# A seven-product MLP with more groups: partial sums seeded into PSUM, kept in DRAM between pieces, and more low parts made by adding transfers

## The chip, the cores and the metric

The kernel runs on one core of one Trainium2 chip. A core has a matrix engine (TensorE, in profiles PE, with PEld for its weight loads), a vector engine (VectorE, DVE), an activation engine (ScalarE, ACT), a general engine (GpSimd, POOL) and a queue engine (SyncE, SP) that here issues most transfers. TensorE adds its products into PSUM, eight banks of 128 x 512 float32 words; everything else lives in SBUF or in DRAM. The metric is the device time of one execution in microseconds; smaller is better.

## The reference

The program is one inference step of a transformer layer for two groups of 128 tokens each, prompt (s = 0) and sample (s = 1), with a model width of 2048:

```
h = RMSNorm(x) * (1 + scale1) + shift1
q_A|k_A|v_A|q_B|k_B|v_B|gate_A|gate_B = split(h @ w_in)
x = x + gate1 * ((sigmoid(gate_A) * (o_A @ w_br_a) + sigmoid(gate_B) * (o_B @ w_br_b)) @ w_out)
h2 = RMSNorm(x) * (1 + scale2) + shift2
x = x + gate2 * (square(relu(h2 @ w_up)) @ w_down)
```

The six shift, scale and gate vectors are `silu(cond) @ w_ada + b_ada`, with one condition vector for each token group. `o_A` and `o_B` are two attentions with 128 cached keys each. `w_up` is 2048 x 8192 and `w_down` 8192 x 2048: the MLP is over half of the work. All inputs and outputs are float32.

## The kernel before

Each weight tile is 128 x 1024 float32 words, 512 KB, and is loaded once. To keep float32 accuracy, every operand is split into a high part (what TensorE's fp32r format holds) and a low part (the rest), and a product is three matmuls: high x high, high x low, low x high. The high part of a weight tile is a copy by ScalarE (`prep_hi`, through `copy`, line 93), the low part a subtraction by VectorE (`prep`, line 241). A few tiles, listed in `LO_DMA`, get their low part otherwise: ScalarE writes the negated high part and a transfer from POOL's queue adds the weight to it in SBUF (`minus_plus`, lines 247 and 248).

The work is a list of 456 steps, `wsteps`, in the order in which TensorE runs them. Steps 0 to 71 are the first columns of `w_in` (nine units of 512 columns, cut along the contraction into the CHUNKS 2, 2, 2, 4, 6 of its 16 tiles, so a unit comes back in each chunk); 72 to 135 the gates; 136 to 167 the branches; 168 to 199 `w_out`; 200 to 215 the first two column tiles of `w_up`. Then come eight pieces. A piece is a *pair*, two column tiles of `w_up` (16 steps; pair p from step 184 + 32p), and a *down* stage, four units of 512 output columns over the two column tiles of the piece (16 steps; down p from 232 + 32p, and down 7 from 440). The pair of the next piece stands ahead of a piece's down stage. A plain step is twelve 128x512 matmuls. Down stage 6 is steps 424 to 439, down stage 7 is 440 to 455.

Within a pair, the eight positions are contraction blocks of 256 rows. A block can be done plainly, in two steps of twelve matmuls, or as a *group of seven products* (a Strassen scheme over 2 x 2 blocks; the two token groups are its rows): an x step and a y step with 21 matmuls in all. `FAST` lists which positions do the latter. A group needs sums of weight tiles (t, u and YB) and their splits, made by `prep_x` and `prep_y` on VectorE and ScalarE. The seven accumulators take all eight banks together with Z, and at the pair's end VectorE adds them up (line 1229).

The down sums of a unit n over the eight pieces are held in SBUF (`dsum[n]`). After each piece the accumulated part is added by VectorE (line 1269), or, where `SUM_DMA` says so, copied by ScalarE and added by a transfer (line 1273). Before the last piece, `gate_sum` multiplies the sum by the gate g2 and adds it to the residual x1 (lines 1250 and 1251); the last piece's part is added by `resid` (lines 916 and 917) and written out.

A *dot* (line 1339) is a column of `silu(cond) @ w_ada` computed on VectorE: a 128 x 1024 tile of the transposed weights times a broadcast condition (`cB`), summed along the row, one operation for each token group. `DOTS2` are the steps after which the 32 tiles of gate g2 are worked on. `gate_rows` transposes the column of dots on TensorE (line 1352), writes it to DRAM, and `gate_bc` reads it back as a broadcast.

The order of every engine's work is what the program text emits step by step, in `run`: first the loads that are due (up to `RUN` steps past the step, each weight `LOAD` = 4 steps earlier still), then the preparation of weights up to `LOOK` steps ahead, then the step's matmuls, then what is listed after that step in `cal`. Each engine works through its own queue in order. Tiles come from one pool of `GEN` buffers of 128 x 1024 words, and a new tile waits for the last reader of the old one.

Of the kernel before, what the change touches and what calls it, by code (L numbers as in the profile page):

```python
# [18 lines left out]
P = 128  # L19
# [11 lines left out]
GEN = 48  # L31
# [15 lines left out]
LOOK = "652422234122454433223333332123333453344534333554455544344534333543324554444555556665556644444333333333332222122312344544555434333333342344333334333323445566643344456656433344434444445455564546555553444554322466554554433333333434334533333333333654544332334455643444555653315536554523333334543233333332223323365455455443222212233432443334434642333334444544534434333333333325434222223333434444444434555642255242433444442233554442233242223342112224442233345544"  # L47
RUN = "300000000000010212223333322222222221111122244455544355434445554334554445555775654544345434444445665543321222222212444444444444442222222232223344444455544544444444555454454466677755566555554543365434343355445756644443566664333312222234552332223333334545332333333333322211133333332233311101234434433332332112444444442454322211333343334323233334544422742222212223445554422333233322222211222333333435767445344121210002232000233455555566567556433435335553333334"
CONST_AT = [67, 70]
XL_DMA = []  # L50
ADA_AT = [None, 4, 13, 16, 21, 36, 32]
XS_AT = {1: 13, 2: 18, 3: 29}
POST = {('kvA', 0): [67, 70, 75], ('qA', 0): [70, 73, 78], ('qA', 1): [72, 74, 80], ('kB', 0): [77, 86, 90], ('qB', 0): [82, 84, 93], ('kB', 1): [87, 92, 95], ('qB', 1): [90, 93, 96]}
JOBS = [[79, 80, 80, 87, 93], [81, 83, 88, 90, 93], [87, 87, 89, 90, 96], [93, 93, 96, 102, 105], [96, 97, 100, 105, 112], [102, 103, 107, 112, 123], [105, 107, 111, 118, 123], [112, 115, 118, 121, 123]]
SS_AT = [41, 57, 73, 75, 135, 139]
T_AT = [4, 4]
PREP_IN = [6, 4]
DOTS = [33, 39, 42, 45, 47, 48, 49, 50, 53, 55, 55, 55, 60, 65, 69, 70, 73, 75, 80, 84, 90, 91, 92, 93, 95, 100, 101, 103, 103, 104, 108, 110, 111, 112, 115, 118, 120, 122, 123, 124, 126, 127, 128, 129, 130, 132, 133, 134, 137, 138, 138, 143, 144, 145, 147, 150, 153, 157, 159, 160, 166, 167, 170, 172, 173, 174, 175, 176, 178, 178, 179, 183]
DOTS2 = [230, 232, 234, 235, 236, 237, 240, 243, 255, 263, 265, 269, 270, 288, 300, 300, 306, 328, 328, 331, 333, 334, 358, 360, 362, 364, 368, 368, 391, 391, 395, 399]
STAT_AT = [-1, 0, 10, 11]  # L60
T_PAIR = [[10, 8], [6, 8], [8, 10], [5, 7], [10, 13], [8, 9], [12, 11]]
P_PAIR = [[5, 2], [2, 4], [3, 5], [-1, 3], [5, 8], [3, 3], [7, 4]]
M_TE = (3,)
M_AT = [1, 3, 8]
FLIP = 1
P_UP = [2, 2]
T_UP = [7, 5]
# [4 lines left out]
def tile_hybrid_step(ctx: ExitStack, tc: tile.TileContext, a):  # L72
# [25 lines left out]


    cols = cp.tile([P, 164], F32, name="cols")  # L100
    act.dma_start(cols, a["cols"])
    xnT = [G(f"xnT{g}").rearrange("p (k s t) -> p k s t", k=4, s=2) for g in range(4)]
    for g in range(4):
        sync.dma_start(xnT[g].rearrange("p k s t -> p (k s t)"), a["xT"][g])
# [1405 lines left out]
```

## Time and profile before

| | |
|---|---|
| median of 3 runs | 1329.3 us (1329.23 to 1330.28) |
| profiled execution: span from its first to its last instruction | 1327.5 us |
| TensorE matmuls busy | 1314.7 us, 6414 instructions |
| VectorE busy | 1179.5 us |
| ScalarE busy | 796.3 us |
| HBM read, written | 365.58 MB, 8.16 MB |

The profiled execution has no time of its own beside its span; the median of the runs is 1.8 us longer, which is what lies around the span. In the page's first part each engine has its busy time, share and count of instructions. In the second the span is cut into 40 slices and each digit is a share in tenths. A row of a group reads: line, engine, operation, output <- inputs, shape, count | busy time in us, mean ns of one | idle time of the engine before it and what ended that. A row of a timeline begins with the start in us and the duration. A row of waits reads: who <- for whom: us in total, times, longest. A row of windows has the stretch, its length, then busy time and instruction count of PE, PEld, DVE, ACT and POOL, the granted clock, the share of the transfer engines and GB/s. A matmul's duration is longer than the distance between two of them, since they are pipelined.

### The profile page before, as it was taken

How to read it: one execution, taken by the hardware profiler on the slowest of the kernel's cores; microseconds unless marked ns; L12 is line 12 of the kernel's file. 1: busy time of each engine (PE TensorE's matmuls, PEld its weight loads, DVE VectorE, ACT ScalarE, POOL GpSimd, SP SyncE). 2: the span in 40 equal slices, each digit the busy share in tenths (PEclk: the TensorE clock that was granted, in tenths of full speed). 3: DMA queues.
4: the chain of work that ended last, by engine and by line, in shares of the span. 5: the costliest groups of instructions: out<-in, count | busy, mean ns of one | idle time of the engine just before them, and what ended most of it. 6: DMA issues, size and time to landing. Idle time of an engine off the chain costs nothing.

```text
span 1327.5 us, 18042 instructions
## 1 busy us (share of the span) xinstructions
PE 1314.7 (99%) x6414; PEld 1066.7 (80%) x6415; DVE 1179.5 (89%) x1529; ACT 796.3 (60%) x973; POOL 49.9 (4%) x61
## 2 busy tenths in 40 slices
PE   8999999999999999999999999999999999999998
PEld 4777788788888878888888888888888888878886
DVE  4588999988898999999779998998999999989595
ACT  5634443467655546645677766767767567676560
POOL 0000000511000000000000000000000000000000
PEclk9999999999999999999999999999999999999999
DMA  9999997978589999996568956988969597788962
GB/s 372 408 409 409 409 387 278 389 263 272 188 310 351 359 390 331 375 370 239 191 229 262 302 222 229 276 290 276 278 223 298 203 305 248 273 224 283 312 208 100
DMA packets 147546, 389.62 MB, mean 294 GB/s; under 512 B 51712, under 2 KB 52928, under 8 KB 147456
## 3 DMA queue, kind: packets, MB, share of 16 engines
q1 hardware_dynamic: 144160, 377.11, 79.0%
q0 software_dynamic: 3152, 11.27, 4.3%
q8 instruction: 50, 0.82, 0.2%
q14 instruction: 40, 0.33, 0.1%
q10 hardware_dynamic: 144, 0.08, 0.0%
HBM read 365.58 MB, written 8.16 MB: 282 GB/s over the span
## 4 chain that ended last, share of the span: by engine, by line
PE 94%; DMA 4%; DVE 1%; ACT 0%; POOL 0%; issue 0%; SPq 0%; ACTq 0%
PE acc L291 17%; PE acc L293 17%; PE acc L292 17%; PE Q L1129 6%; PE Q L1131 6%; PE Q L1130 6%; PE acc L394 4%; PE acc L395 4%; PE acc L396 4%; DMA araw<-in_w_pair 3%; PE ps_ada L308 2%; DMA raw<-in_w_in 1%; PE Z L1129 1%; PE Z L1131 1%; PE Z L1130 1%; PE ps_S L719 1%
## 5 line engine op out<-in xcount | busy, mean ns | idle before, releaser
L241 DVE TENSOR_TENSOR wL<-raw,wH 128x1024 fp32r<-128x1024 f32 x379 | 449.9, 1224 | 62.4 <-ACT wH L93 58.0
L93 ACT ACTIVATE wH<-raw 128x1024 fp32r<-128x1024 f32 (+1 forms) x395 | 394.5, 1044 | 129.5 <-PE acc L396 21.5
L394 PE MATMUL acc<-wH,hH 128*128 128x512 f32 x276 | 109.1, 395 | 0.0
L396 PE MATMUL acc<-wH,hL 128*128 128x512 f32 x276 | 107.5, 390 | 0.0
L395 PE MATMUL acc<-wL,hH 128*128 128x512 f32 x276 | 107.5, 390 | 0.0
L291 PE MATMUL acc<-wH,hH 128*128 128x512 f32 x256 | 101.3, 396 | 0.0
L293 PE MATMUL acc<-wH,hL 128*128 128x512 f32 x256 | 99.7, 390 | 0.0
L292 PE MATMUL acc<-wL,hH 128*128 128x512 f32 x256 | 99.7, 389 | 0.0
L1339 DVE CUSTOM_DVE_ANT_0 junk<-aT,cB,cols 128x1024 bf16<-128x1024 f32 x56 | 71.7, 1286 | 0.0
L1339 DVE CUSTOM_DVE_ANT_0 aT<-aT,cB,cols 128x1024 f32<-128x1024 f32 x56 | 71.4, 1281 | 0.2
L93 ACT ACTIVATE tH<-t 128x1024 fp32r<-128x1024 f32 x32 | 33.9, 1060 | 51.9 <-DVE t L1184 44.5
L394 PEld LDWEIGHTS acc<-wH,hH 128*128 128x128 f32 x276 | 51.8, 188 | 13.6 <-issue 2.9
L396 PEld LDWEIGHTS acc<-wH,hL 128*128 128x128 f32 x276 | 51.8, 188 | 11.0
L395 PEld LDWEIGHTS acc<-wL,hH 128*128 128x128 f32 x276 | 51.9, 188 | 10.3
L293 PEld LDWEIGHTS acc<-wH,hL 128*128 128x128 f32 x256 | 48.1, 188 | 10.1
L291 PEld LDWEIGHTS acc<-wH,hH 128*128 128x128 f32 x256 | 48.1, 188 | 9.8 <-ACT wH L93 0.4
L292 PEld LDWEIGHTS acc<-wL,hH 128*128 128x128 f32 x256 | 48.1, 188 | 9.4
L93 ACT ACTIVATE uH<-raw 128x1024 fp32r<-128x1024 f32 x32 | 34.0, 1063 | 30.0 <-DVE raw L1189 29.0
L1235 ACT ACTIVATE up<-up 128x1024 f32<-128x1024 f32 x28 | 29.7, 1062 | 28.3 <-DVE up L1229 27.9
L308 PE MATMUL ps_ada<-araw,cpad 128*32 128x256 f32 x640 | 39.3, 382 | 2.6 <-DMA araw<-in_w_pair 2.5
L93 ACT ACTIVATE fTa<-pTa 128x2048 uint16<-128x2048 uint16 x16 | 40.5, 2534 | 2.1 <-PE acc L293 1.5
L1184 DVE TENSOR_TENSOR t<-raw 128x1024 f32<-128x1024 f32 x32 | 39.1, 1221 | 2.9 <-PE Q L1131 1.7
(641 smaller groups left out, 3291.7 us busy)
## 6 DMA issues: line engine op xcount, KB each, us to landing
raw<-in_w_in SPq DMA_DIRECT2D x133, 512.0 KB, 9.5
raw<-in_w_down SPq DMA_DIRECT2D x128, 512.0 KB, 5.7
araw<-in_w_pair SPq DMA_DIRECT2D x80, 512.0 KB, 10.0
aT<-in_w_gT SPq DMA_DIRECT2D x64, 512.0 KB, 6.8
raw<-in_w_up SPq DMA_DIRECT2D x64, 512.0 KB, 5.1
raw<-in_w_upF SPq DMA_DIRECT2D x64, 512.0 KB, 5.3
aT<-in_w_adaT SPq DMA_DIRECT2D x48, 512.0 KB, 9.9
raw<-in_w_out SPq DMA_DIRECT2D x32, 512.0 KB, 10.3
```

The source lines that it names most:

```text
L93: act.activation(out, in_, AF.Copy)
L241: dve.tensor_tensor(st["lo"], st["raw"], st["hi"].bitcast(F32), op=OP.subtract)
L291: pe.matmul(acc[tb], sh, wh[:, k, :], start=f, stop=False)
L292: pe.matmul(acc[tb], sh, wl[:, k, :], start=False, stop=False)
L293: pe.matmul(acc[tb], sl, wh[:, k, :], start=False, stop=l)
L394: pe.matmul(acc[tb], sh, wh[:, k, :], start=kt == 0 and k == 0 and not held, stop=False)
L395: pe.matmul(acc[tb], sh, wl[:, k, :], start=False, stop=False)
L396: pe.matmul(acc[tb], sl, wh[:, k, :], start=False, stop=last and k == 1 and not hold)
L1129: pe.matmul(acc, stat[0], hi, start=f, stop=False)
L1130: pe.matmul(acc, stat[0], lo, start=False, stop=False)
L1131: pe.matmul(acc, stat[1], hi, start=False, stop=l)
L1339: dve.tensor_tensor_reduce(out, box["raw"], cB[s, tag], 1.0, dst if second else baT[:, part, fb:fb + 1], OP.mult, OP.add, dst)
```

## The change

- Each of the seven pairs gets six groups of seven products (positions 0, 2, 3, 5, 6, 7): 42 groups in place of 32.
- The down units 1, 2 and 3 no longer add to a sum in SBUF. Between pieces their sums are written to DRAM by POOL's queue (up to piece 5), read back by SP's queue, and copied by ScalarE into the two PSUM banks of the unit (`seed`) before its matmuls, which then add to them. The last two pieces hand the sum over in SBUF. Unit 0 is added by VectorE as before, and only it goes through `gate_sum`.
- In the input projection, the units of chunks 3 and 4 (but the two that stay open) are seeded likewise from their partial sums.
- The high part of a weight is made one step ahead of its low part (`prep_a`, `prep_b`, HI_AHEAD), also in the groups; high and low parts of transposed tiles are made a step apart (JOIN_LO).
- `LO_DMA` has 35 entries in place of 10. One, 230, is the x step of a group, which makes its own parts in `x_hi` and `x_lo`; 34 are plain steps.
- The silu of the condition is computed once, at the start, and kept in DRAM; `cB` is read from there.
- The g2 dots are ordered by down unit, and each unit's gate is transposed and broadcast by itself (`gate_row2`, `gate_bc2`, through POOL's queue). Sixteen of the 32 dots now stand at steps 424 to 444.
- Some small constants move into two general buffers (`early`), and `GEN` grows from 48 to 50. The step lists (LOOK, RUN, DOTS, POST, JOBS and others) are new.

```diff
-GEN = 48
+GEN = 50
-DOTS1 = [11, 15, 27, 29, 29, 30, 32, 35]
+DOTS1 = [26, 26, 29, 36, 39, 40, 41, 42]
-FAST = {1: (0, 3, 7), 2: (0, 4, 5, 7), 3: (0, 2, 4, 5, 7), 4: (0, 2, 4, 5, 7), 5: (0, 3, 4, 5, 7), 6: (0, 2, 5, 6, 7), 7: (0, 1, 3, 5, 7)}
-SUM_DMA = [5, 6, 11, 13, 16, 19, 21, 23, 25]
+FAST = {1: (0, 2, 3, 5, 6, 7), 2: (0, 2, 3, 5, 6, 7), 3: (0, 2, 3, 5, 6, 7), 4: (0, 2, 3, 5, 6, 7), 5: (0, 2, 3, 5, 6, 7), 6: (0, 2, 3, 5, 6, 7), 7: (0, 2, 3, 5, 6, 7)}
+SUM_BACK = 8
+SEED_IN = {3: -1, 4: 0}
+SEED_N = (1, 2, 3)
+HI_AHEAD = 1
+JOIN_LO = 1
+SEED_AT = 3
+GATE2_USE = 3
+ROW_AT = [5, 5, 9, 5]
-LO_DMA = [89, 107, 131, 176, 184, 233, 292, 314, 319, 404]
+LO_DMA = [88, 106, 116, 131, 165, 180, 184, 196, 218, 224, 230, 232, 250, 251, 256, 282, 283, 288, 314, 315, 320, 329, 346, 347, 352, 378, 379, 384, 392, 410, 416, 442, 443, 449, 450]
...
-ADA_AT = [None, 4, 13, 16, 21, 36, 32]
+ADA_AT = [None, 5, 13, 16, 21, 37, 32]
-DOTS2 = [230, 232, 234, 235, 236, 237, 240, 243, 255, 263, 265, 269, 270, 288, 300, 300, 306, 328, 328, 331, 333, 334, 358, 360, 362, 364, 368, 368, 391, 391, 395, 399]
+DOTS2 = [234, 237, 240, 266, 269, 272, 298, 301, 329, 330, 332, 363, 364, 367, 397, 398, 424, 426, 426, 428, 429, 431, 431, 432, 432, 436, 439, 439, 440, 441, 444, 444]
...
+    act.activation(crow[:, 1, :], crow[:, 0, :], AF.Sigmoid)
+    pool.tensor_tensor(crow[:, 1, :], crow[:, 0, :], crow[:, 1, :], op=OP.mult)
+    pool.dma_start(silu, crow[:, 1, :])
...
-    prep_next = [0]
+    prep_next = [0, 0]
     def prep_to(end):
-        while prep_next[0] < min(len(wsteps), end):
-            prep(wsteps[prep_next[0]])
-            prep_next[0] += 1
+        for q, (ahead, fn) in enumerate(((HI_AHEAD, prep_a), (0, prep_b))):
+            while prep_next[q] < min(len(wsteps), end + ahead):
+                fn(wsteps[prep_next[q]])
+                prep_next[q] += 1
...
+    def seed(box, src):
+
+        box["acc"] = [bank("acc", pacc) for _ in range(2)]
+        for tb in range(2):
+            copy(box["acc"][tb], src[:, tb, :])
...
+            seed_step = len(wsteps) - nk // 2 + SEED_IN[c] if c in SEED_IN and j >= 2 else None
+            start_steps(u, k0, nk, c > 0 and j < 2, c < ends and j >= nf - 2, seed_step)
...
-    def unit(w, c0, ktiles, stat, evac, key, order="both"):
+    def unit(w, c0, ktiles, stat, evac, key, seed_from=None):
...
+        if seed_from:
+            at(len(wsteps) - SEED_AT, lambda: seed(box, seed_from()))
...
+            def x_hi(b=b):
+                b["X"] = b["x"].pop("raw")
                 b["XH"] = G("XH", F32R)
-                copy(b["XH"], b["x"]["raw"])
+                copy(b["XH"], b["X"])
+
+            def x_lo(b=b):
+                b["XL"] = G("XL", F32R)
+                dve.tensor_tensor(b["XL"], b["X"], b["XH"].bitcast(F32), op=OP.subtract)
...
+            def y_split(b=b):
+                for n, v in (("t", b["t"]), ("u", b["Y"])):
+                    b[n + "H"], b[n + "L"] = G(n + "H", F32R), G(n + "L", F32R)
+                    copy(b[n + "H"], v)
+                    dve.tensor_tensor(b[n + "L"], v, b[n + "H"].bitcast(F32), op=OP.subtract)
...
+    def sum_back(p, n):
+        dsum[n] = G(f"dsum{n}").rearrange("p (s n) -> p s n", s=2)
+        sync.dma_start(dsum[n].rearrange("p s n -> p (s n)"), sum_mem[p - 1, n])
+
     def down_unit(p, n):
+        seeded = p > 0 and n in SEED_N
+        if seeded and p < last:
+            load_at(len(wsteps) - SUM_BACK, lambda: sum_back(p, n))
+
         def evac(acc):
-            by_pool = 4 * p + n in SUM_DMA
-            if p == 0 or by_pool:
+            whole = p == 0 or seeded
+            if whole and p != last:
                 part = G(f"dsum{n}").rearrange("p (s n) -> p s n", s=2)
             for s in range(2):
                 if p == last:
                     out_s(acc, n, s)
-                elif p == 0 or by_pool:
+                elif whole:
                     copy(part[:, s, :], acc[s])
                 else:
                     dve.tensor_tensor(dsum[n][:, s, :], dsum[n][:, s, :], acc[s], op=OP.add)
-            if p == 0:
+            if n in SEED_N and p < last - 1:
+                sum_mem[p, n] = dp.tile([P, 1024], F32, name=f"sm{p}{n}")
+                pool.dma_start(sum_mem[p, n], part.rearrange("p s n -> p (s n)"))
+            elif whole and p != last:
                 dsum[n] = part
-            elif by_pool:
-                pool.dma_start(dsum[n], part, accum_op=OP.add)
...
+    def gate_row2(n):
+
+        ps = bank("ps_gr")
+        pe.transpose(ps[0:8, 0:P], g2col[n].rearrange("p s k -> p (s k)"), ident)
+        row = sp.tile([P, 512], F32, name="grow", tag="S", bufs=2)[0:8, 0:P]
+        copy(row, ps[0:8, 0:P])
+        grow["g2", n] = dp.tile([8, P], F32, name=f"gr_g2{n}")
+        pool.dma_start(grow["g2", n], row)
+
+    def gate_bc2(n):
+
+        gbc["g2", n] = G(f"g2_{n}").rearrange("p (s n) -> p s n", s=2)
+        rows = grow["g2", n].rearrange("(s k) f -> s (k f)", s=2)
+        for s in range(2):
+            pool.dma_start(gbc["g2", n][:, s, :], rows[s:s + 1, :].partition_broadcast(P))
...
+        for n in range(4):
+            i = DOTS2[(15, 15, 23, 31)[n]] + ROW_AT[n]
...
+            ex(i, lambda n=n: gate_row2(n))
+            e = end_of(("down", last, n)) - (GATE2_USE if n == 0 else 0)
...
+            ex(max(i + 1, e - 12), lambda n=n: gate_bc2(n))
+            load_at(e - 6, lambda n=n: x1_back(n))
```

In the new LOOK, the steps of the pairs have the value 4 and those of the down stages 5 almost everywhere, between 2 and 8 from step 416 on; the new RUN is 5 or 6 there. In LOOK, steps 0 to 15 are `6523224141224543` (before `6524222341224544`); in RUN they are `4111111111111213` (before `3000000000000102`).

More of the change, by code (lines that the diff above doesn't have):

```diff
@@ L281, in run, with mm3 @@
                 fn()
-    def mm3(acc, stat, st, first, last, order=(0, 1)):
+    def mm3(acc, stat, st, first, last, seeded=False):
         wh, wl = st["hl"]
@@ L1409, in tile_hybrid_step @@
     assert i + 1 <= end_of(("out", 2)), (i, end_of(("out", 2)))
[L1410 to L1420 removed]
+    dots2()
     e = end_of(("out", 3))
```

229 lines of the change are left out of this document (126 added, 103 removed).

## The prediction

> **What bounds the kernel now.** I read the page first (busy time, the slices), then TensorE's waits, then its timeline for the true pace of a matmul, then stretches of the end.
>
> ```profile
> span 1327.5 us, 18042 instructions
> PE 1314.7 (99%) x6414; PEld 1066.7 (80%) x6415; DVE 1179.5 (89%) x1529; ACT 796.3 (60%) x973; POOL 49.9 (4%) x61
> DVE  4588999988898999999779998998999999989595
> PEclk9999999999999999999999999999999999999999
> DMA  9999997978589999996568956988969597788962
> q1 hardware_dynamic: 144160, 377.11, 79.0%
> q0 software_dynamic: 3152, 11.27, 4.3%
> ```
>
> TensorE is at work 99% of the span at a full clock. VectorE and the transfers are both above 80%, so neither can take much more work. What TensorE waits for, and its pace:
>
> ```profile
> PE ps_ada L308 <- DMA araw<-in_w_pair: 2.5, 5, 0.6
> PE acc L473 <- ACT hH L93: 1.3, 2, 0.9
> PE ps_gr L1352 <- DVE gc_g L1339: 1.0, 1, 1.0
> ...
> 699.99 0.39 PE L1129 MATMUL Q<-wH,h22H 128*128 128x512 f32 x1
> ...
> 712.23 0.39 PE L1129 MATMUL Q<-wH,h22H 128*128 128x512 f32 x1
> ```
>
> The waits come to under 10 us. Between the two matmuls quoted there are 54 starts: 12.24 / 54 = 0.2267 us each. That is the price of a 128x512 matmul here; 0.39 us is its pipelined length. Twelve of them, a plain step, last 2.72 us. TensorE's chain is nearly gapless, so time can be won by removing matmuls, and lost where something that is late makes new gaps.
>
> **The change, part by part.**
>
> *Matmuls.* FAST goes from 3+4+5+5+5+5+5 = 32 groups to 7 x 6 = 42. A group of seven products is 7 x 3 = 21 matmuls, a plain one 24. Ten more groups remove 30: 30 x 0.2267 = **-6.8 us**, all on the path. (The Trainium skill, TensorE: Matmul & The Clock Gate, section "Wait — 56ns, not 53.3ns?", gives N / 2.4 GHz + 2.5 ns, 215.7 ns for 512 columns; by it the sum would be -6.5. The trace has 226.7 ns and decides.)
>
> *VectorE in all.*
>
> ```profile
> L241 DVE TENSOR_TENSOR wL<-raw,wH 128x1024 fp32r<-128x1024 f32 x379 | 449.9, 1224 | 62.4 <-ACT wH L93 58.0 <-issue 2.3 <-DMA araw<-in_w_pair 1.5
> L1184 DVE TENSOR_TENSOR t<-raw 128x1024 f32<-128x1024 f32 x32 | 39.1, 1221 | 2.9 <-PE Q L1131 1.7 <-PE Z L1130 0.6 <-DMA raw<-in_w_upF 0.5
> L1187 DVE TENSOR_TENSOR raw<-t,raw 128x512 f32<-128x512 f32 x32 | 22.1, 692 | 1.2
> L1269 DVE TENSOR_TENSOR dsum<-dsum,acc 128x512 f32<-128x512 f32 x30 | 19.6, 685 | 3.3 <-PE acc L293 3.2
> L406 DVE TENSOR_TENSOR u_kB<-u_kB,acc 128x512 f32<-128x512 f32 x12 | 7.8, 683 | 2.6 <-PE acc L396 2.6
> L1322 DVE TENSOR_TENSOR cB<-cB,sgB 128x1024 f32<-128x1024 f32 x10 | 12.1, 1223 | 1.0 <-ACT sgB L1321 1.0
> L1339 DVE CUSTOM_DVE_ANT_0 aT<-aT,cB,gc_g 128x1024 f32<-128x1024 f32 x32 | 40.7, 1283 | 0.2
> ```
>
> A fast group costs VectorE four full operations and three halves, 4 x 1.22 + 3 x 0.69 = 6.95; a plain one two, 2.45. Ten more: +45.0. Low parts by transfer, 34 that are used against 10: -24 x 1.22 = -29.4. Sums of the down units: 12 adds in place of 30, -12.3; gate_sum for one unit in place of four, -12 x 0.69 = -8.3. Seeds in the input projection: 14 units x 2 adds, -19.1. The ten silu products: -12.1. Together -36: VectorE falls from 1179 to about 1143 us. It pays for the ten groups, but only over the whole span.
>
> *ScalarE.*
>
> ```profile
> L93 ACT ACTIVATE wH<-raw 128x1024 fp32r<-128x1024 f32 (+1 forms) x395 | 394.5, 1044 | 129.5 <-PE acc L396 21.5 <-PE acc L292 17.9 <-DVE wL L241 15.5
> L93 ACT ACTIVATE dsum<-acc 128x512 f32<-128x512 f32 x26 | 15.1, 595 | 18.5 <-PE acc L293 17.8
> ```
>
> It gains 25 negated copies (+26), 10 x 1.6 for the groups (+16), 70 seed copies, 28 evacuations in their place and 18 more sums (116 x 0.6 = +69), and loses ten sigmoids (-10): about 900 us, 68%. No row shows a copy into PSUM. Reading PSUM takes 0.60 and SBUF half-size copies about the same; I take 0.60, and between nothing and twice that ScalarE still stays below 75%. A seed is emitted after the third step before its unit, so two plain steps (5.4 us) cover its two copies. Without that cover each of the 35 would cost up to 1.2 us. The sums come back from DRAM on SP's queue, SUM_BACK 8 plus RUN 5 or 6 steps ahead of their unit, over 35 us, against some 9 for a landing; were one late, the seed would wait in ScalarE's queue and the high parts behind it with it.
>
> Down unit 3 is now always evacuated by ScalarE, and the pair behind it needs its banks. Before, that was so in four of seven places, and in one it showed:
>
> ```profile
> 942.78 1.06 ACT XH L93
> 943.85 0.49 ACT dsum L93
> 944.38 0.50 PE Q L1129
> ```
>
> There a high part ran ahead of the evacuation and TensorE's next product came 0.2 us late. Three more such places are 0 to 0.6 us: nothing is charged.
>
> *The pairs.* Six fast groups and two plain ones are 39.4 us of TensorE. VectorE's own pace shows here:
>
> ```profile
> 1188.13 1.22 DVE L1184 TENSOR_TENSOR t<-raw 128x1024 f32<-128x1024 f32 x1
> ...
> 1194.73 1.22 DVE L1184 TENSOR_TENSOR t<-raw 128x1024 f32<-128x1024 f32 x1
> ...
> 1302.93 6.90 DVE L241 TENSOR_TENSOR wL<-raw,wH 128x1024 fp32r<-128x1024 f32 x6
> ```
>
> One group takes 6.6 us, one plain low part (6.90 - 1.22) / 5 = 1.14. A pair needs 6 x 6.6 + 1 or 2 x 1.14 + about 5 for the sums at its end = 46, 7 us more than TensorE gives. The down stage after it (43.5 us of TensorE) needs some 28, so it gives back 15; LOOK keeps 4 to 6 steps prepared ahead, 11 to 16 us. The high parts go a step earlier still (HI_AHEAD) and the low parts of the transposed tiles a step later (JOIN_LO), which moves work and adds none. I charge nothing here. If the lead were gone, each pair would cost up to 7.
>
> *Start.* The first pair of modulation columns is used one step later (ADA_AT 4 to 5), which gives its loads 2.7 us more; the 2.5 us of waits for them can shrink by about 1.5. But split_h now lies directly ahead of step 9, which reads it, with four preparations queued before it. I set +1 to +2 against -1.5: zero. The dots that stood at steps 11 and 15 move to 26.
>
> *Gate rows.* Four transposes in place of one for g2: three more at 0.28 and a weight load of 0.1, +1.1 us. The 1.0 us wait of the one of before goes for the first two, whose dots end at 399 and which stand at 403. What is late next is the last row, below.
>
> *The last two down stages (steps 424 to 455).* DOTS2 puts 16 of 32 dots, two VectorE operations each, at 424 to 444; before, the last stood at 399.
>
> ```profile
> 1235.50:1290.00 54.50, 54.50 (x242) 45.15 (x241) 38.81 (x44) 40.15 (x39) 0.86 (x1) 1.00 0.83 263
> 1290.00:1322.50 32.50, 32.50 (x145) 26.72 (x143) 21.46 (x27) 3.18 (x3) 0.00 (x0) 1.00 0.27 100
> 40.00:200.00 160.00, 159.10 (x981) 123.49 (x982) 138.71 (x207) 71.63 (x90) 0.00 (x0) 1.00 1.02 404
> ...
> 1154.96 1.28 DVE L1339 CUSTOM_DVE_ANT_0 junk<-aT,cB,gc_g 128x1024 bf16<-128x1024 f32 x1
> ...
> 1156.17 1.28 DVE L1339 CUSTOM_DVE_ANT_0 junk<-aT,cB,gc_g 128x1024 bf16<-128x1024 f32 x1
> ```
>
> The first row is steps 424 to 443: VectorE 38.8 of 54.5 us. Added are 14 dots x 2 x 1.21 = 33.9; removed two gate_sums (-5.2), four sums (-2.4) and two low parts (-2.3): 62.8, that is 8.3 too many. Preparation five steps ahead (13.6 us) covers it with 5 left. The last dots, at 444 and 445, end by the same reckoning about when their row stands, at 449: between no wait and 3 us.
>
> *Transfers there.* At 404 GB/s, 512 KB take 1.30 us of all 16 engines; the software queue's 4.3% (57 us) less its five plain writes, over 19 adding transfers, gives 2.8 us each.
>
> ```profile
> raw<-in_w_down SPq DMA_DIRECT2D x128, 512.0 KB, 5.7
> wL<-in_w_down POOLq DMA_DIRECT2D x2, 512.0 KB, 9.0
> g<-gr_g SPq DMA_DIRECT2D x16, 256.0 KB, 8.3
> L1273 POOL DMA_DIRECT2D dsum<-dsum x9: 859/859/867, 838.5 to 1258.3; - x9
> ```
>
> The same window holds 0.83 x 54.5 = 45 us of them. Added: 14 dot tiles 18, four adding transfers 11, the saved rows and gates that come later 6; removed one adding transfer 3. So 77 in 54.5, 22 too many. The weights are issued 9 or 10 steps ahead (RUN 5 or 6 plus LOAD 4), 25 to 27 us, of which landing takes 5.7 and the two preparations 2.2: 17 to 19 remain, less than 22 by 3 to 5 at the worst moment, while the window's share before it can lend some. I take **+2 us** of stall for the stretch, bounds 0 and 10. POOL's queue issues each transfer in 0.86 us, in order, behind a copy by ScalarE; the low part of step 443 is started at 438, 13.6 us ahead, and needs 1.9 + 0.9 + 9.0: it lands 2 us early when nothing queues. Over the whole span the transfers go from 83% to 91%: 25 adding (+70, one of them for step 230, whose low part nothing reads), nine fewer sums (-25), 36 trips of sums through DRAM (+47), four more cB tiles (+5).
>
> **The sum**, against the profile's own span: 1327.5 - 6.8 (matmuls) - 1.0 (gate row's wait) + 1.1 (rows) + 2 (last stretch) + 0 (start) = 1322.8. The runs' median is 1.8 us above the span: **1324.6 us**.
>
> **The rivals.** (a) Clean: the stretch's lead holds and the start wins its 1.5: 1329.3 - 6.8 - 1.0 + 1.1 - 1.5 = 1321. For it: VectorE lost 58 us waiting for ScalarE's high parts (row L241), and they now go a step earlier. (b) Late dots: VectorE is 5 us late at the end, the last row's transpose holds TensorE for 3 and the gate's write and read back (8.3 us to land) delay the last outputs by 1 or 2: 1327.5, within the band. (c) Slower: transfers bind in steps 417 to 447. With 30 too many in place of 22 the weights are 30 - 18 = 12 us late: 1324.6 + 10 = 1335. It decides from 27 on, where the stall passes 9. Against it: the first 200 us run at a share of 1.02 with TensorE 159.1 of 160 busy. The Trainium skill (DMA: Bandwidth & Descriptors, section "Where 436 GB/s comes from") lets HBM to SBUF bind at about 358 GB/s; by it the overload would be about 32 and the time some 1337. The 404 GB/s of the row speaks against that. (d) The pairs become VectorE's: the ten groups win nothing and each pair pays 5 to 7: about 1360. Against it: before, the pair with five groups and several dots beside them had as much to do, and TensorE's waits list nothing of it.
>
> **How the numbers follow.** Chances: forecast 0.42, (a) 0.21, (b) 0.17, (c) 0.17, (d) 0.03. A measurement of this kernel tells about 0.2% (2.7 us) from no change. Faster than 1326.6: forecast and (a), 0.63; within: (b), 0.17; slower: (c) and (d), 0.20. The range runs from 1319 (the clean case with two us more of removed waits) to 1333, which takes in the lower third of (c); by itself the forecast spans 1322 to 1327.
>
> **What would show it.** 6414 - 30 + 3 = 6387 matmuls and VectorE near 1143 us. No waits of TensorE in the pairs. In the window of the last two down stages: VectorE above 95%, the transfers' share near 1, and a wait of ps_gr for gc_g of under 3 us. The prediction is wrong if TensorE waits for weights, for seeds, or for a low part by transfer by more than 5 us in all.

## The result and the profile after

The changed kernel takes 1324.3 us (median of 5 runs, 1322.7 to 1326.2), the kernel before 1329.3 (1329.2 to 1330.3) beside it: a ratio of 0.996, with a 95% interval of 0.9948 to 0.9973, so 0.3 to 0.5% faster. The forecast was 1324.6. The profiled execution has a span of 1322.5 us against 1327.5. From the page of the changed kernel:

```profile
span 1322.5 us, 18220 instructions
PE 1309.0 (99%) x6388; PEld 1061.3 (80%) x6388; DVE 1151.4 (87%) x1487; ACT 890.8 (67%) x1129; POOL 87.1 (7%) x109
...
q1 hardware_dynamic: 146128, 386.54, 80.1%
q0 software_dynamic: 8848, 31.23, 10.3%
```

TensorE still fills 99% of the span. VectorE is down by 28 us, ScalarE up by 95, and the software queue's share has gone from 4.3 to 10.3%. What TensorE waits for (who <- for whom: us in total, times, longest):

```profile
PE acc L314 <- DMA wL<-in_w_down: 1.7, 1, 1.7
PE ps_ada L330 <- DMA araw<-in_w_pair: 1.3, 2, 0.7
...
PE acc L315 <- DVE a14L L890: 1.1, 1, 1.1
...
PE ps_gr L1424 <- DVE gc_g L1411: 0.3, 1, 0.3
```

The first and third rows are new, and both lie in the last two down stages. No wait for an operand of the pairs (XL, uL, tL) is listed. The table gives the length of each stage in both kernels, from the first 128x512 matmul of the stage to the first of the next in the two timelines:

| stage | before, us | after, us | difference |
|---|---|---|---|
| up to pair 1 | 689.79 | 688.87 | -0.92 |
| pair 1 (3 groups -> 6) | 41.48 | 39.44 | -2.04 |
| pair 2 (4 -> 6) | 40.80 | 39.44 | -1.36 |
| pairs 3, 5, 6, 7 (5 -> 6), each | 40.12 | 39.44 | -0.68 |
| pair 4 (5 -> 6) | 40.46 | 39.44 | -1.02 |
| down stages 0 to 4, each | 43.52 to 43.58 | 43.52 | -0.07 in all |
| down stage 5, with the first gate rows | 44.80 | 43.80 | -1.00 |
| down stage 6 | 43.52 | 43.94 | +0.42 |
| down stage 7, to the last matmul | 43.29 | 46.93 | +3.64 |
| after the last matmul's start | 5.17 | 5.26 | +0.09 |

The rows add up to -5.0. Ten groups bring 10 x 0.68 = 6.8 us, and the last two down stages give 4.1 back. The windows of the changed kernel show why these two are special (stretch, length, then busy time and count of PE, PEld, DVE, ACT, POOL, the granted clock, the share of the transfer engines, GB/s); the first row is pair 1, the last two are down stage 6 with the start of 7, and the rest of 7:

```profile
688.90:728.30 39.40, 39.40 (x175) 32.64 (x174) 37.43 (x42) 33.70 (x38) 2.59 (x3) 1.00 0.95 292
...
1226.35:1280.80 54.45, 52.85 (x231) 42.58 (x229) 54.31 (x76) 39.22 (x42) 3.96 (x6) 1.00 1.05 357
1280.80:1317.50 36.70, 35.45 (x156) 29.03 (x156) 29.87 (x42) 14.82 (x19) 5.00 (x8) 1.00 0.72 230
```

In the second row VectorE is busy for 54.31 of 54.45 us, the share of the transfers is 1.05, and TensorE misses 1.6 us. The chain of waits that ends the kernel names the step by which it got there:

```profile
1264.93 7.43 issue
1272.37 9.64 DMA wL<-in_w_down
1282.05 0.50 PE acc L314
```

The low part of step 443 is started by POOL at 1272.37 and lands 9.64 us later, when TensorE has stood for it. POOL had been idle for 7.4 us before, until ScalarE had written the negated high part (1272.08 in ScalarE's timeline, which shows what held it):

```profile
1266.39 2.56 ACT L101 ACTIVATE fTa<-pTa 128x2048 uint16<-128x2048 uint16 x1 [1.62 <-DMA pTa<-pla]
...
1269.95 1.04 ACT L101 ACTIVATE wH<-raw 128x1024 fp32r<-128x1024 f32 x1
1271.02 1.06 ACT L266 ACTIVATE wL<-wH 128x1024 fp32r<-128x1024 f32 x1
...
1281.53 0.27 ACT L101 ACTIVATE grow<-ps_gr 8x128 f32<-8x128 f32 x1 [5.64 <-issue]
1281.70 1.09 ACT L101 ACTIVATE acc<-dsum 128x512 f32<-128x512 f32 x2
```

The transposed planes (pTa) came late by transfer, and the high part of step 443 stands behind their copy. The same planes make a14H and a14L, the operand of the other new wait. The fourth row is a second thing: the gate row's copy out of PSUM stood for 5.64 us, and the seeds of the next unit stand behind it. It writes into a tile of a size class with two slots (`tag="S"`), which the unused outputs (junk) of VectorE's dots take too.

### The profile page after: what moved, and what is told of

Same layout as the page of the kernel before. It is cut to its first block, busy times and chain, and to the rows that moved or that the text cites. A ratio compares the mean times of both kernels' runs of the same rounds, so it can differ in the third digit from the quotient of the medians.

```text
span 1322.5 us, 18220 instructions
## 1 busy us (share of the span) xinstructions
PE 1309.0 (99%) x6388; PEld 1061.3 (80%) x6388; DVE 1151.4 (87%) x1487; ACT 890.8 (67%) x1129; POOL 87.1 (7%) x109
## 3 DMA queue, kind: packets, MB, share of 16 engines
q1 hardware_dynamic: 146128, 386.54, 80.1%
q0 software_dynamic: 8848, 31.23, 10.3%
## 4 chain that ended last, share of the span: by engine, by line
PE 93%; DMA 3%; DVE 2%; issue 1%; POOL 0%; ACT 0%; POOLq 0%; DVEq 0%; ACTq 0%
PE acc L313 16%; PE acc L314 16%; PE acc L315 16%; PE Q L1191 6%; PE Q L1192 6%; PE Q L1193 6%; PE acc L424 5%; PE acc L425 5%; PE acc L426 5%; PE ps_ada L330 2%; DMA araw<-in_w_pair 2%; PE ps_S L756 1%; DMA wL<-in_w_down 1%; DVE aT L1411 1%; PE acc L1026 1%
## 5 line engine op out<-in xcount | busy, mean ns | idle before, releaser
L101 ACT ACTIVATE wH<-raw 128x1024 fp32r<-128x1024 f32 (+1 forms) x376 | 381.0, 1045 | 126.4 <-DMA raw<-in_w_in 17.0
L260 DVE TENSOR_TENSOR wL<-raw,wH 128x1024 fp32r<-128x1024 f32 x335 | 399.1, 1223 | 47.8 <-ACT wH L101 32.7
L1256 DVE TENSOR_TENSOR tL<-t,tH 128x1024 fp32r<-128x1024 f32 x42 | 51.2, 1220 | 11.2 <-ACT tH L101 11.2
L101 ACT ACTIVATE uH<-raw 128x1024 fp32r<-128x1024 f32 x42 | 44.4, 1058 | 23.6 <-DVE raw L1250 21.5
L425 PEld LDWEIGHTS acc<-wL,hH 128*128 128x128 f32 x276 | 51.9, 188 | 10.3
L101 ACT ACTIVATE tH<-t 128x1024 fp32r<-128x1024 f32 x42 | 44.3, 1054 | 23.5 <-DVE t L1246 18.5
L1246 DVE TENSOR_TENSOR t<-raw 128x1024 f32<-128x1024 f32 x42 | 51.2, 1218 | 1.0 <-PE acc L314 1.0
L1238 DVE TENSOR_TENSOR XL<-raw,XH 128x1024 fp32r<-128x1024 f32 x42 | 51.2, 1218 | 0.6 <-DMA sm<-dsum 0.5
L1256 DVE TENSOR_TENSOR uL<-raw,uH 128x1024 fp32r<-128x1024 f32 x42 | 51.1, 1218 | 0.0
```

What stands on the lines that cost most here:

```text
L101: act.activation(out, in_, AF.Copy)
L260: dve.tensor_tensor(st["lo"], st["raw"], st["hi"].bitcast(F32), op=OP.subtract)
L425: pe.matmul(acc[tb], sh, wl[:, k, :], start=False, stop=False, **kw)
L1256: dve.tensor_tensor(b[n + "L"], v, b[n + "H"].bitcast(F32), op=OP.subtract)
```

## The experiments

Two theories were to be told apart at first. A: VectorE's backlog from the 16 late dots makes the loss of 4 us. B: the transfers are overloaded there, and what arrives late (planes, the low part by transfer) makes it. After that: whether the pairs owe their clean run to the relief, and whether a version without the loss can be had.

**The low part of step 443 by VectorE.**

```diff
-LO_DMA = [..., 416, 442, 443, 449, 450]
+LO_DMA = [..., 416, 442, 449, 450]
```

> The changed kernel with step 443 taken out of LO_DMA: its low part is a VectorE subtraction (1.14 us) again. In the changed kernel's profile TensorE waits 1.7 us for that low part by transfer, at 1280 us. If the lateness of this one transfer is a loss of its own, the wait goes and the span falls by 1 to 1.7 us. If VectorE, which is gapless there (54.31 of 54.45 us busy), is the real bound, the added 1.14 us comes back as a wait for a VectorE low part or a gate row and the span moves by less than 0.5 us.

Measured: 1323.1 us (1322.8 to 1323.7), ratio 0.9957 (0.9942 to 0.9972). In the waits of this kernel, from step 424 on, the row of the transfer is gone and others stand in its place:

```profile
PE acc L313 <- ACT acc L101: 1.1, 2, 0.6
PE acc L315 <- DVE a14L L890: 0.5, 1, 0.5
```

Down stage 6 is 1.0 us longer than in the changed kernel and stage 7 is 1.6 shorter. So the wait for the transfer can be removed, but more than half of it comes back as waits for seeds. The median lies 1.1 us below that of the changed kernel, but the intervals of the two ratios overlap almost wholly, so a gain is not shown.

**The transposed planes two steps earlier.**

```diff
-T_PAIR = [..., [8, 14], [12, 9]]
+T_PAIR = [..., [8, 14], [10, 9]]
```

> The changed kernel with the joining of the transposed tile a14 two steps earlier (T_PAIR's last pair [10, 9] in place of [12, 9]). TensorE waits 1.1 us for a14L at 1270 us in the changed kernel. If it is late only because it stands late in VectorE's queue, the wait goes and the span falls by about 1 us. If the transposed planes themselves come late (ScalarE waited 1.6 us for that transfer), ScalarE is held two steps earlier, high parts behind it come later, and the gain is under 0.5 us or negative.

Measured: 1330.4 us (1329.4 to 1331.2), ratio 1.001 (1.000 to 1.0019). The longest of the waits of this kernel:

```profile
PE acc L314 <- DMA wL<-in_w_down: 4.3, 1, 4.3
```

The wait for a14L is gone, but the work that needs the planes is asked for earlier while the planes come no earlier, so ScalarE stands for them with the high parts behind it, and the low part of step 443 is 4.3 us late in place of 1.7. Seven starts at half the pace behind that wait (last section) add 1.4 us, and smaller waits for other operands make most of the rest of the 6.1. A wait on an in-order queue that is moved ahead costs whatever stands behind it.

**The late dots cut to 8 words, their tiles still loaded** (the gates of down units 2 and 3 are then sums over 8 words).

```diff
+        n = 8 if tag[0] == "c" else 1024
-        dve.tensor_tensor_reduce(out, box["raw"], cB[s, tag], 1.0, ...
+        dve.tensor_tensor_reduce(out[:, 0:n], box["raw"][:, 0:n], cB[s, tag][:, 0:n], 1.0, ...
```

> The changed kernel with VectorE's part of the last 16 dots cut to 8 of 1024 words (their 512 KB tiles are still loaded; the gates of down units 2 and 3 come out wrong). It takes some 32 x 1.1 = 35 us of VectorE work out of the last two down stages and leaves the transfers. If VectorE is what makes the last stretch late (4 us over the unhindered pace, of which 3.1 us are waits), the waits for a14L and the gate row go, and the span falls by 1.5 to 3 us. If the transfers are, all waits stay and the span moves by less than 0.5 us.

Measured: 1324.4 us (1322.7 to 1325.6), ratio 0.9964 (0.9954 to 0.9974). The window and the first wait of this kernel:

```profile
1226.35:1280.80 54.45, 52.94 (x234) 43.08 (x233) 33.15 (x86) 40.42 (x45) 4.51 (x7) 1.00 1.04 353
```

```profile
PE acc L314 <- DMA wL<-in_w_down: 1.5, 1, 1.5
```

VectorE has 21 us less to do there, the wait for a14L is gone, and the low part by transfer is as late as before. The share of the transfers is unchanged at 1.04. The profiled execution has a span of 1320.9 us, 1.6 below the changed kernel's, but it is the fastest of nine, and the median of the runs is that of the changed kernel: what the wait for a14L is worth does not show in the median.

**The late dots computed, their tiles not loaded** (they multiply the broadcast condition by itself, so these gates are other numbers).

```diff
+        late = tag[0] == "c"
-        out = box["raw"] if s else sp.tile([P, 1024], BF16, name="junk", tag="S", bufs=2)
+        out = box["raw"] if s and not late else sp.tile([P, 1024], BF16, name="junk", tag="S", bufs=2)
+        src = cB[s, tag] if late else box["raw"]
...
+            if tag != "c":
-                load_at(i - 2, lambda box=box, fb=fb, h=h: dot_load(box, ("g2", fb), h))
+                load_at(i - 2, lambda box=box, fb=fb, h=h: dot_load(box, ("g2", fb), h))
```

> The changed kernel with the tiles of the last 16 dots not loaded (the dots run at full length on the condition tile in their place; the gates of down units 2 and 3 come out wrong). It takes 16 x 1.3 = 21 us of transfers out of the last stretch and leaves VectorE's work. If the overloaded transfers (share 1.05 there) make it late, the waits for the low part of step 443 and for a14L go and the span falls by 2 to 3 us, with a share near 0.7. If VectorE does, they stay.

Measured: 1327.0 us (1326.8 to 1328.5), ratio 0.9986 (0.9977 to 0.9996). Window, waits and ScalarE's timeline of this kernel:

```profile
1226.10:1280.60 54.50, 53.33 (x235) 43.59 (x234) 54.27 (x75) 37.18 (x40) 3.75 (x6) 1.00 0.82 260
```

```profile
PE acc L313 <- ACT acc L101: 3.3, 1, 3.3
...
PE acc L315 <- DVE a14L L890: 1.2, 1, 1.2
```

```profile
1262.54 2.53 ACT L101 ACTIVATE fTa<-pTa 128x2048 uint16<-128x2048 uint16 x1
...
1284.83 0.27 ACT L101 ACTIVATE grow<-ps_gr 8x128 f32<-8x128 f32 x1 [12.82 <-issue]
```

With the share down to 0.82 the planes are in time, the copy fTa starts 3.9 us earlier without a wait, and the wait for the low part of step 443 is gone. The wait for a14L stays, with VectorE at 54.27 of 54.50. Together with the run before, as the two profiled executions show it: the two new waits have two causes. VectorE's backlog makes a14L late, and the transfers make the low part of step 443 late; neither theory alone explains both. And the time got worse, by the slot: every dot of the last stretch now takes a slot for both token groups, the row's copy stood for 12.8 us, and the seeds behind it held TensorE for 3.3. Seven starts at half the pace followed (last section), which is 1.4 us more.

**The gate row's copy in a buffer of its own class.**

```diff
-        row = sp.tile([P, 512], F32, name="grow", tag="S", bufs=2)[0:8, 0:P]
+        row = G("grow")[0:8, 0:P]
```

> The changed kernel with one edit: the tile into which ScalarE copies a gate row out of PSUM comes from the general buffers, not from the two slots that the unused outputs of VectorE's dots also take. In the changed kernel that copy stood 5.6 us in ScalarE's queue with the seeds of the last unit but one behind it. Theory that the shared slot costs something by itself: the copy runs when its transpose is done (about 1277.5 in place of 1281.5), the seeds follow, and the time falls by 0.3 to 1.5 us (1323 to 1324). Rival: TensorE was held by the low part of step 443 anyway (1.7 us at 1280), the seeds were in time behind it, and the time stays at 1324.3 within 0.5.

Measured: 1324.5 us (1323.8 to 1325.4), ratio 0.9964 (0.9951 to 0.9976). ScalarE's timeline and TensorE's waits:

```profile
1278.25 0.27 ACT L101 ACTIVATE grow<-ps_gr 8x128 f32<-8x128 f32 x1 [1.05 <-PE ps_gr L1440]
```

```profile
PE acc L313 <- DVE up L1291: 0.7, 1, 0.7
PE acc L314 <- DMA wL<-in_w_down: 0.6, 1, 0.6
```

The copy now waits for its transpose alone and runs 3.3 us earlier: the shared slot was the cause of its wait. But the time doesn't move. The low part of step 443 costs 1.1 us less, and a wait of 0.7 for the pair's last sums (up) appears, while a14L's goes from 1.1 to 1.2.

**Own slot, and neither step 443 nor the unread 230 by transfer.**

> The changed kernel with the own slot for the gate row and without the transfers for the low parts of steps 443 and 230; dots where the change put them. Without step 443 by transfer alone, 1.1 us of waits for the seeds were left, behind the row's copy. Theory that these two add up: the seeds' wait goes, what is left is a14L's 0.5 to 1.1, time 1321.5 to 1323, below every kernel so far. Rival: VectorE, gapless there, is what the last stretch lasts as long as (its 1.2 us more for the low part come back as another wait), and the time stays at 1323 to 1324.5.

Measured: 1324.6 us (1323.7 to 1326.5), ratio 0.9966 (0.9955 to 0.9976); the rival held. From step 424 on, the waits of this kernel:

```profile
PE acc L315 <- DVE a14L L890: 1.2, 1, 1.2
PE acc L313 <- DVE up L1291: 1.1, 1, 1.1
```

What is left is VectorE's. Of the six edits to the last stretch so far, four land within 1.2 us of the changed kernel. In three of these, one wait goes or shrinks and another shows or grows; with the short dots a wait goes and none comes, and the median stays all the same.

**The dots spread out: four to each of down stages 0 to 5 and eight in the last two**, with the two edits above.

```diff
-DOTS2 = [234, 237, 240, 266, 269, 272, 298, 301, 329, 330, 332, 363, 364, 367, 397, 398, 424, ... 444]
+DOTS2 = [234, 236, 238, 240, 266, 268, 270, 272, 298, 300, 302, 304, 330, 332, 334, 336, 362, 364, 366, 368, 394, 396, 398, 400, 425, ... 439]
```

> The changed kernel with three edits for its last stretch: the 32 gate dots four to a down stage and eight in the last two (in place of 16), the tile that takes the gate row out of PSUM in a buffer of its own size class instead of the two slots that the dots' unused outputs also take, and the low part of step 443 (and the unread one of 230) not by transfer. Theory (VectorE's backlog, the overloaded transfers and the shared slot together cost the 4 us that the last two down stages lost): the waits there go, 1320 to 1322. Rival: the dots that now stand in earlier down stages take the lead of the pairs behind them, and the time stays at 1324 or rises to 1330.

Measured: 1327.4 us (1326.9 to 1329.1), ratio 0.9987 (0.9978 to 0.9996). Window of pair 7 in this kernel, and its longest wait:

```profile
1188.40:1232.40 44.00, 41.40 (x175) 33.75 (x175) 39.79 (x41) 31.00 (x33) 1.44 (x2) 0.96 0.92 318
```

```profile
PE Q L1191 <- ACT dsum L101: 2.6, 1, 2.6
```

The time is the rival's. Down stage 7 is clean (43.4 us), but pair 7 takes 44.0 us in place of 39.4 and down stage 6 takes 44.5. The pairs up to pair 5 are unharmed. The loss of pair 7 is this one wait, for ScalarE's evacuation of a down unit, and eight starts at half the pace behind it (1.6 us, last section). What delayed the evacuation stands ahead of it in ScalarE's queue:

```profile
1188.43 2.52 ACT L101 ACTIVATE fTa<-pTa 128x2048 uint16<-128x2048 uint16 x1 [2.66 <-PE acc L314]
```

This copy writes a general buffer, and so waits for the last reader of the old tile, here a matmul. VectorE was busy for 39.79 of the 44.00 us. The dots' tiles take general buffers too, so that the earlier dots use up buffers is an explanation beside a lead of VectorE that is used up; neither is shown.

**A half measure: 4, 4, 4, 3, 3, 2 dots ahead, twelve in the last two stages**, with the same two edits.

> The changed kernel with the own slot for the gate row, the low part of step 443 not by transfer (nor the unread one of 230), and four of the 32 dots moved out of the last two down stages into down stages 0 to 3: 4, 4, 4, 3, 3, 2 ahead of them and 12 in them (16 before this edit). Theory that VectorE's backlog, the transfers and the slot make the loss of 4 us together, and that an early down stage has room for a fourth dot where the one before the last two has none: pairs of 39.44 us as in the changed kernel, last two down stages 43.5 and 44 to 45, time 1320.5 to 1322. Rival (the fourth dots use up the lead, as the four in down stage 5 did for the last pair): a pair above 40 us and 1324 or more.

Measured: 1327.8 us (1325.3 to 1329.6), ratio 0.9989 (0.998 to 0.9998), the rival again. Pairs 5 and 6 take 40.2 us each, pair 7 41.6 and down stage 6 48.0. The kernel with the same two edits and the dots left in place takes 1324.6, so moving the dots costs 3 us: earlier stages have no room for even four more. No version was found that is faster than the changed kernel beyond the noise.

**The 42 groups alone, in the kernel before.**

```diff
-FAST = {1: (0, 3, 7), 2: (0, 4, 5, 7), 3: (0, 2, 4, 5, 7), ...
+FAST = {1: (0, 2, 3, 5, 6, 7), 2: (0, 2, 3, 5, 6, 7), 3: (0, 2, 3, 5, 6, 7), ...
-LO_DMA = [89, 107, 131, 176, 184, 233, 292, 314, 319, 404]
+LO_DMA = [89, 107, 131, 176, 184, 233, 314, 404]
```

> The kernel before with the 42 groups alone: its dots, sums, seeds and low parts stay where they were (two low parts by transfer fall away, since their steps are now parts of a group). My theory: the ten groups take 6.8 us from TensorE, but VectorE gets 45 + 2 x 1.2 = 47 us more (1179.5 to about 1227) and nothing in return, so the pairs with dots beside them run out of lead; waits of TensorE for the low parts and sums of the pairs of 5 to 25 us in all, time 1328 to 1348. Rival: the lead of 4 to 6 steps carries the ten groups by itself, no wait of TensorE above 0.5 us in the pairs, time 1322 to 1323, and all other parts of the change were not needed for it.

Measured: 1368.5 us (1365.5 to 1369.1), ratio 1.0286 (1.0269 to 1.0303). Waits, and the window of pair 1:

```profile
PE Q L1130 <- DVE XL L1192: 14.2, 9, 2.9
PE Q L1130 <- DVE uL L1194: 8.4, 7, 1.3
PE acc L291 <- DVE up L1229: 5.5, 3, 3.7
```

```profile
690.30:739.10 48.80, 41.21 (x175) 31.98 (x174) 41.37 (x43) 36.23 (x40) 0.94 (x1) 1.00 0.63 212
```

The same ten groups that bring 6.8 us in the changed kernel cost 39 here. Pair 1 takes 48.8 us, against 39.4 in the changed kernel, for the same matmuls. So the rest of the change carries the groups; which part of it, the next runs ask.

**The preparations' lead of before, from step 208 on** (a mean of 3.5 steps in place of 4.5, taken over steps 208 to 455; in the new LOOK a pair has mostly 5 in its first eight steps and 4 in the others, a down stage 4 and then 5).

```diff
-LOOK = "...32266766666666566655544444444444444445555..."
+LOOK = "...32266665545544333333334343345333333333336..."
```

> The changed kernel with the lead of the preparations (LOOK) of the kernel before from step 208 on: a mean of 3.6 steps in place of 4.6 ahead of use; groups, seeds, sums, dots and transfers as changed. Theory that the lead of 4 to 6 steps is what lets the six groups of a pair pass: waits of TensorE for XL and uL in the pairs, each pair longer by 2 to 8 us, time 1335 to 1370. Rival: the work taken from VectorE (sums, seeds, low parts by transfer, dots moved to the end) does it, and the shorter lead costs at most 3 us: 1324 to 1327.

Measured: 1345.0 us (1343.2 to 1346.2), ratio 1.0115 (1.01 to 1.0131): 21 us slower than the changed kernel by one string of digits. Pair 1 takes 47.3 us and pair 4 takes 43.4, the other five between 39.4 and 40.2, and down stage 6 takes 51.9 in place of 43.9: some 13.5 of the 21 us are lost in the pairs and 8 in that stage. Two of the waits, one of the pairs and the longest of the last stretch:

```profile
PE acc L314 <- DVE wL L260: 4.5, 2, 3.4
PE Q L1192 <- DVE uL L1256: 2.9, 4, 1.3
```

The lead is a necessary part. It isn't all: with the short lead and the relief 21 us are lost, with the short lead and no relief 44 (1368.5 against 1324.3, the old order of preparations included). What the order (HI_AHEAD, JOIN_LO), the seeds, the sums in DRAM and the two more buffers bring, each by itself, was not tried.

**Ten low parts by adding transfers in place of 34.**

```diff
-LO_DMA = [88, 106, 116, 131, 165, 180, 184, ... 416, 442, 443, 449, 450]
+LO_DMA = [88, 106, 131, 180, 184, 232, 288, 314, 320, 392]
```

> The changed kernel with 10 low parts by adding transfers in place of 34: 24 go back to VectorE (24 x 1.22 = 29.3 us, VectorE about 1180), the transfers lose 24 x 2.8 = 67 us of the 16 engines. Theory that the adding transfers pay for the groups: TensorE waits for low parts made by VectorE in several down stages, 1327 to 1340. Rival, that the seeds, sums and silu (39 us taken from VectorE) were enough and the adding transfers only load the queues: at most 1325, and in the last two down stages the wait for a low part by transfer is gone.

Measured: 1331.7 us (1329.3 to 1332.4), ratio 1.0014 (1.0005 to 1.0023). Page, waits:

```profile
PE 1308.5 (99%) x6387; PEld 1061.1 (80%) x6388; DVE 1177.6 (89%) x1511; ACT 865.4 (65%) x1103; POOL 66.0 (5%) x84
q0 software_dynamic: 5248, 18.12, 4.8%
```

```profile
PE acc L314 <- DVE wL L260: 3.3, 1, 3.3
PE acc L313 <- ACT acc L101: 1.7, 1, 1.7
```

Both sides were partly right. Down stage 6 begins at 1226.41 us, in the changed kernel at 1226.35: up to there the extra adding transfers bring nothing at all, though VectorE has 26 us more to do in the whole. The loss of about 5 us in the span lies in the last two down stages, where four of the 24 were (442, 443, 449, 450). That these four alone would do was not tried.

**Seven groups more, 49.**

```diff
-FAST = {1: (0, 2, 3, 5, 6, 7), ...
+FAST = {1: (0, 2, 3, 4, 5, 6, 7), ...
```

> The changed kernel with seven groups more, 49 (the nine low parts by transfer whose steps become parts of groups, or that stood beside them, fall away). TensorE loses 7 x 3 matmuls, 21 x 0.2267 = 4.8 us; VectorE gains 7 x 4.5 + about 8 x 1.22 = 41 us, about 1192. If what is left in the pairs is TensorE's pace, the time is 1324.3 - 4.8 = 1319.5 (each pair 0.68 us shorter). If the pairs with six groups were already at VectorE's limit, a pair with seven (7 x 6.6 + 1.1 + 5 = 52 us of VectorE against 38.8 of TensorE) uses up the lead and waits appear in the last pairs: 1326 to 1345.

Measured: 1367.8 us (1367.2 to 1370.4), ratio 1.0292 (1.0276 to 1.0307). Nine low parts by transfer fall away with it. The longest item of the waits, and pairs 1 and 2:

```profile
PE Q L1192 <- DVE XL L1238: 19.8, 13, 2.4
```

```profile
688.84:738.50 49.66, 42.00 (x172) 32.80 (x171) 45.67 (x53) 33.62 (x38) 0.87 (x1) 0.97 0.71 232
782.04:827.25 45.21, 41.16 (x172) 32.98 (x171) 44.59 (x49) 27.23 (x31) 0.56 (x1) 0.96 0.77 265
```

One group more in each pair, and the pair falls from TensorE's pace to that of its preparation: 49.7 us for pair 1 and 42.6 to 45.2 for the others, where the matmuls are 39.44 - 0.68 = 38.8. In pair 2 this is VectorE's pace, busy for 44.59 of 45.21 us. In pair 1 VectorE still had 4 us without work, so there it is not VectorE's busy time alone. Six groups stand at the edge.

## Why the prediction was right, and where its terms were off

*Matmuls, -6.8: right.* The distance of 0.2267 us and 30 matmuls give the ten steps of 0.68 in the table to the hundredth.

*VectorE, ScalarE, transfers.* Forecast were 1143 us, 900 and 91%. The pages have 1151.4, 890.8 and 80.1 + 10.3 = 90.4% of the two queues. An adding transfer was priced at 2.8 us of the 16 engines; the run with 25 fewer gives (10.3% x 1322.5 - 4.8% x 1327.5) / 25 = 2.9. A seed copy was taken at 0.60, without a row; ScalarE's timeline shows two in 1.09 us. VectorE's busy time lies 8 us above the forecast. About 3 are the wL row: 379 operations became 335 and the row fell by 50.8 us, 1.15 each, where the working took off 1.224 each. The other 5 are overlap: the rows of all lines together fall by 33 us (1257.9 to 1224.8), while the page, which counts overlapping operations once, falls by 28.

*Pairs, nothing: right in the sum, and the margin was overstated.* All seven are 39.44 us with no wait. The text named the lead of 4 to 6 steps, 11 to 16 us, as the cover, and said that each pair would cost up to 7 without it. The run with the old lead bears the cover out: one pair lost 7.9 us, another 4.0. But by the same reckoning a pair of seven groups lacks 52 - 38.8 = 13 us, which such a lead should nearly have covered, and the pairs lost 10.9 (the first) and 3.8 to 6.4 (the others). What speaks against rival (d) in the text, that the pairs of before had as much to do, was no argument: that kernel with six groups loses 39 us.

*Start, zero: it was -0.9.* The waits for the modulation's tiles shrank from 2.5 to 1.3 us, as reckoned, and the charge of 1 to 2 for split_h did not come: that wait is 1.3 us in both kernels.

*Gate rows, -1.0 and +1.1: the first right, the second too dear.* The stage with the first row lost the 1.0 us though it now has two of them. One of the later rows in TensorE's timeline:

```profile
1276.90 0.39 PE L315 MATMUL acc<-wH,a14L 128*128 128x512 f32 x1
1277.12 0.27 PE L1440 MATMUL ps_gr<-ident,gc_g 128*8 128x128 f32 x1
...
1277.47 0.40 PE L314 MATMUL acc<-wL,a15H 128*128 128x512 f32 x1
```

Between the two ends lie the row's transpose and one more matmul. From 1276.90 to 1277.47 are 0.57 us where two plain distances are 0.45: a row costs 0.12 us. The working had added its length of 0.28 and a weight load; but a matmul's length is not its distance, as the text itself had said of the 128x512 ones. Three rows are 0.4.

*The bank wait of 0.2 us:* in place of more of them, the ones of before went: 0.34 in pair 4 and 0.06 in down stage 2.

*The last two down stages, +2 with bounds 0 and 10: the place and the state right, the size 3.8 (4.1 with its two gate rows), and the way in which it comes wrong.* VectorE was to be above 95% (54.31 of 54.45), the transfers near 1 (1.05), the row's wait under 3 us (0.3). But TensorE waited for no weight itself. Of the new waits one is the step that the text gave 2 us of margin, the low part of step 443: it took ScalarE's copy and negation to be made within 1.9 us of the start of step 438, but that step starts at 1264.85 and they end at 1272.08, after 7.2 us, behind the copy of the late planes. The other, a14L behind VectorE's dots, was not in the text, which charged the dots to the gate row alone. Both waits cost more than their rows say: the starts around the 1.7 lie 2.08 us apart and the next 0.33, where two plain distances are 0.45, so TensorE loses 1.96.

*The sum.* The terms that were off: start -0.9, bank waits -0.4, gate rows -0.9 (three rows 0.4 in place of 1.1, and the wait that went, with the second row in its stage, 1.1 in place of 1.0), last stretch +1.8, the end +0.1. Together that is -0.3, the distance from 1324.6 to 1324.3; the agreement is better than the working, since errors of 0.4 to 1.8 us cancel. The 1.8 us around the span held (1324.3 - 1322.5).

## What to carry to other kernels

A cut in the bounding engine's work is worth its full price only while the next engine still has a lead: the same ten groups brought 6.8 us with one step more of lead and some relief, and cost 39 without. Where two resources are full in one stretch at the end of a kernel, taking away one late operand shows the next one; move work out of the stretch only to places whose slack you have measured, since four dots moved to earlier stages cost 3 us more than they saved. Look also at which small tiles share a ring of slots: a wait of one engine for another can come from there and hold everything queued behind it.

## What the runs showed of the hardware

A wait of TensorE can cost more than itself, by the clock. In the half measure's kernel, TensorE's timeline after a wait of 2.53 us (the one before it, of 1.31 us, had ended 7.4 us earlier):

```profile
1233.58 0.50 PE L313 MATMUL acc<-wH,a12H 128*128 128x512 f32 x1 [2.53 <-DVE up L1291]
...
1234.87 0.63 PE L314 MATMUL acc<-wL,a12H 128*128 128x512 f32 x1
1235.30 0.63 PE L315 MATMUL acc<-wH,a12L 128*128 128x512 f32 x1
```

For some 3 us the starts lie 0.43 us apart in place of 0.227, seven distances that cost 1.4 us, and the granted clock of the ten microseconds around is 0.83:

```profile
1230.00:1240.00 10.00, 7.47 (x26) 5.63 (x25) 9.76 (x14) 5.81 (x8) 1.12 (x2) 0.83 1.03 407
```

In the kernel before with 42 groups the span is 40 us longer though 6.8 us of matmuls are gone, so 47 us are to be accounted for. From the first pair on, its timeline has 21 waits of 29 us in all, and the starts around them lie 33 us further apart than plain ones. Another 43 distances are of the slow kind, which is 43 x 0.2 = 9 us more; its mean granted clock is 0.989. The other 5 us are small gaps and the 0.5 us up to pair 1. The Trainium skill (TensorE: Matmul & The Clock Gate, section "Wait — 56ns, not 53.3ns?") gives 426.7 ns between starts of 512 columns at the half clock, and the trace agrees. The section "What's actually happening" puts the fall to an idle window of about 3.4 us. Here a wait of 2.5 us was followed by it, and one of 3.35 us, in the run with ten low parts by transfer, was not, as the first starts after that wait show:

```profile
1302.95 0.50 PE L314 MATMUL acc<-wL,a14H 128*128 128x512 f32 x1 [3.35 <-DVE wL L260]
...
1303.98 0.39 PE L315 MATMUL acc<-wH,a14L 128*128 128x512 f32 x1
1304.21 0.39 PE L313 MATMUL acc<-wH,a14H 128*128 128x512 f32 x1
```

In all fourteen kernels, from the first pair on, TensorE waited thirteen times for 2 us or more. Slow starts followed ten of these within 3 us, and did not follow three (2.44, 2.72 and 3.35 us); seven more slow stretches came behind shorter waits close together, such as 1.55 and 1.31 us that ended 2.3 us apart in the kernel with 49 groups. So the length of one wait does not decide it; what does is not shown.

The runs of the changed kernel also spread wider than those of before, 3.5 us against 1.1. That this comes from the stretch with the share of 1.05 is an idea only: the one run without the low part of step 443 by transfer spread 0.9 us, but with an own slot beside it 2.8.
